# One hybrid decoder layer: where five key tiles, the first gathered rows and the last norm rows stand around the end of the gate table

## The chip, the core and the metric

The kernel runs on one core of one Trainium2 chip. The metric is the device time in microseconds (us) of one execution, as a median of several. TensorE does the matrix products, VectorE (DVE in the rows) elementwise work, ScalarE (ACT) activations and casts, GpSimd (POOL) issues the gathers, and SyncE (SP) issues most of the other transfers. Each engine works through its own queue in order; what an instruction needs from another engine it waits for at its place in that queue, and everything behind it waits too.

## The reference

The input is 512 tokens of 1024 features. The layer mixes the tokens in two ways (a gated linear recurrence and trailing means), adds the result to the residual stream and normalises it to `h`. Then comes the part that the change touches, a channel mixer that looks up experts:

```python
q = (x @ w_query)                       # per head two half queries
sc = einsum(q, sub_keys)                # 8 heads x 2 halves x 128 keys
top_v, top_i = top_k(sc, 16)            # per half, then the best 16 of the sums
expert = i1 * 128 + i2                  # 16384 experts, 8 x 16 = 128 of them per token
gate = softmax(best_v)
act = gelu(einsum('td,tkd->tk', x, u_tab[expert])) * gate
y = einsum('tk,tkd->td', act, v_tab[expert])
h = LN2(alpha*h + y + ple)
```

`u_tab` and `v_tab` are 16384 x 1024 in float32. `ple` is a gated projection of a second input.

## The kernel before

All products are done as three matmuls of split operands (a high part `wh` and the rest `wl`, in a float32 form that TensorE takes): ScalarE casts `wh` from the loaded tile `wraw` (L219), VectorE subtracts to get `wl` (L220), and `mm3` issues lines 123, 124 and 125.

The 512 tokens are four blocks. The first block (NG = 1) gathers its experts' rows: GpSimd fetches, for each of its 128 experts per token, one row per token with an indirect transfer (`issue`, L967), and VectorE multiplies it with `hg` and sums (`consume`, L978, for `u_tab`), later scales and adds (L981, for `v_tab`). The list `todo` has 128 + 128 such steps. The other three blocks (ND = 384 tokens) compute densely over all 16384 experts, as NT = 128 tiles of 128 experts: a key tile is 8 x 3 matmuls of a `u_tab` tile against the tokens (names `fp`), a gelu, a product with the gates (`weigh`, L1003), and 18 matmuls with the `v_tab` tile into six accumulators (`yacc`).

The gates have to be scattered into a dense table `Gd` (24 groups of 16 tokens). That is the loop `for s in range(nq)`, L925, of 96 steps. A step does one `quad` (12 small matmuls, name `pG`, L890) whose operands `oh` and `A` VectorE builds for two quads at a time (`one_hots`, L870 and L876); ScalarE copies the result to a staging tile `stg` (`evacuate`, L897), and after every fourth quad SyncE writes the group to `Gd` in HBM (L899). Every fourth step also advances `selects()` (the choice of experts of the next block on VectorE, names `eq`, `si`, `eidx`), and eight steps do a `base` (L919). Between the quads the loop spreads the key tiles 15 to 51 (`more_u`): `want = left * (s + 1) // nq`, with `left` = 37 tiles x 8 pieces of three matmuls. Their gelu results are parked in HBM (`Hs`, L643).

Behind the loop come `g_load(order[0])`, which reads one slice of the table back, the gates of eight key tiles (`gt`, L666; it needs every group of `Gd`), and the stage with the value products: `LEAD` = 6 key tiles ahead, then for each tile i the load, the key product of tile i + 6, 18 value matmuls, and a share of gathered rows, `budget += len(todo) * ...`, so that the rows are used up near the end.

What sets the order: in this part of the program the instructions stand on every engine as the Python code emits them. `fetch` (L211) loads weight tiles six ahead of the one in use and splits them three ahead; there are three buffers for `wraw` and four for `wh` and `wl`. The pool `vt` has four large buffers that `stg`, the gathered `rows` (two steps in one buffer), and the gain and bias of the last norm (`gain_bias(2)`, names `gb`, L96, L1010) share. At the start of the last stage the kernel before issues `GL` = 4 gathers (L1052).

Of the kernel before, what the change touches and what calls it, by code (L numbers as in the profile page):

```python
# [15 lines left out]
OP = mybir.AluOpType  # L16
# [5 lines left out]
NCK = 8  # L22
# [8 lines left out]
TG = 16  # L31
VG = 8
NG = 1
ND = S - NG * 128
T0 = NG * 128
NS = 52
PRE = 15
UQ = [0, 0, 0] + [1, 0] * 6 + [1]
UP = [1, 1, 1, 0]
TAIL = 4  # L40
OG = 8
NC2 = 60
CS = 2
EARLY = 4
LEAD = 6
# [6 lines left out]
def hybrid_block(ctx, tc, ins, out, dbg=None):  # L52
    nc = tc.nc
# [29 lines left out]
    hres = persist.tile([128, NB, D], FT, name="hres")  # L83
# [5 lines left out]
    def big(name):  # L89
        return vt.tile([128, 4, S], FT, name=name, tag="vt")  # L90
# [88 lines left out]
    order = list(range(NS, NS + VG))  # L179
# [452 lines left out]
    def flush():  # L632
        while late:
            late.pop(0)()
# [14 lines left out]
    def more_u(n):  # L649
        for _ in range(n):  # L650
            if next(spills, 1) is None:
                done[0] += 1
# [9 lines left out]
    def g_load(e, pool):  # L662
# [4 lines left out]
            gts[j] = gt  # L667
        return gts[j][:, :, (e % VG) * TG:(e % VG + 1) * TG]

    with ExitStack() as pb:  # L670
        rt = pb.enter_context(tc.tile_pool(name="rt", bufs=1))
        eqp = pb.enter_context(tc.tile_pool(name="eqp", bufs=3))
# [252 lines left out]
        for s in range(nq):  # L925
            p = quad(s)
            flush()
            if prev:
                evacuate(s - 1, prev)
            prev = p  # L930
            if s % PACE[0] in PACE[1]:
                next(sels, None)
            elif s % 8 == 7 and s < 64:
                base(s // 8)
            if s % (OG // 4) == 0 and s // (OG // 4) + 1 < ND // OG:
                one_hots(s // (OG // 4) + 1)
            want = left * (s + 1) // nq
            more_u(want - given)
            given = want
        evacuate(nq - 1, prev)  # L940
        for _ in sels:
            pass
        g_load(order[0], g0p)
        more_u(NS * NCK)
        flush()


    with ExitStack() as pc:
# [1 line left out]
        gp = pc.enter_context(tc.tile_pool(name="gp2", bufs=3))  # L950
        yacc = [bank("yacc") for _ in range((NB - NG) * 2)]
        gs, acts, vals = {}, {}, {}

        todo = [(0, b, k) for b in range(NG) for k in range(128)] + [(1, b, k) for b in range(NG) for k in range(128)]
        half_n = len(todo) // 2
        got, cnt, pair = {}, [0, 0], [None]

        def issue():
            n = cnt[0]
            if n >= len(todo):  # L960
                return
            kind, b, k = todo[n]
            if n % 2 == 0:
                pair[0] = big("rows").rearrange("p (a b) c -> p a (b c)", a=2)
            r = pair[0][:, n % 2, :]
            got[n] = r
            nc.gpsimd.indirect_dma_start(out=r, out_offset=None, in_=ins["v_tab" if kind else "u_tab"],  # L967
                                         in_offset=bass.IndirectOffsetOnAxis(ap=eidx[:, b, k:k + 1], axis=0))
            cnt[0] += 1

        def consume():
            n = cnt[1]
            if n >= len(todo) or n not in got:
                return
            kind, b, k = todo[n]
            r = got.pop(n)
            if kind == 0:
                nc.vector.scalar_tensor_tensor(r, r, 1.0, hg[:, b, :], op0=OP.mult, op1=OP.mult,  # L978
                                               accum_out=hdot[:, b, k:k + 1])
            else:  # L980
                nc.vector.scalar_tensor_tensor(hres[:, b, :], r, ggate[:, b, k:k + 1], hres[:, b, :],  # L981
                                               op0=OP.mult, op1=OP.add)
            cnt[1] += 1

        def key_load(i):
            if i < NT:
# [20 lines left out]
                acts[i] = split(vs, gs.pop(i), ND, "a", nc.vector)  # L1007

        lnp = pc.enter_context(tc.tile_pool(name="ln2p", bufs=2))
        g2, b2 = gain_bias(2)  # L1010
        lns = {}

        def finish(blk, half):
# [35 lines left out]
            key_product(i)  # L1049
            weigh(i)  # L1050
        split_act(0)
        GL = 4  # L1052
        for _ in range(GL):
            issue()
        share, tot = 0.0, sum(2 if e >= NS else 1 for e in order[:NT - TAIL - EARLY])
        budget = 0.0
        wait_n = 0
        for i in range(NT):
            key_load(i + LEAD + 1)
            split_act(i + 1)  # L1060
            key_product(i + LEAD)
            vals[i] = take()
            if i < NT - TAIL:
                for b in range(NB - NG):
                    values(i, b)
                acts.pop(i), vals.pop(i)
            budget += len(todo) * (2 if order[i] >= NS else 1) / tot
            while budget >= 1:
                budget -= 1
                if cnt[1] == half_n and wait_n < 2:  # L1070
                    if wait_n == 0:
                        nc.scalar.activation(hdot, hdot, AF.Gelu)
                        nc.vector.tensor_mul(ggate, ggate, hdot)
                    wait_n += 1
                    continue
                consume()
                issue()
            weigh(i + LEAD)
            if i == NT - TAIL - 1:
                while cnt[1] < len(todo):  # L1080
                    consume()
                    issue()
                for blk in range(NG):
                    for half in range(2):
                        finish(blk, half)
                    close(blk)
# [64 lines left out]
```

## Time and profile before

| | us |
|---|---|
| median of 3 runs | 1815.38 (1810.57 to 1819.29) |
| the profiled execution, its own time | 1821.71 |
| span of the profiled execution | 1820.0 |
| TensorE busy | 1759.8 |
| VectorE busy | 1302.0 |
| gate loop, first to last quad | 693.7 to 937.6 |

The views used are the page (busy time of each engine), the table of windows (busy time of the engines, granted TensorE clock and DMA share in a stretch, with the number of instructions behind an x), the groups of instructions by line, the chain of work that ended last, and the timelines of single engines. Times inside the execution are counted from the span's start.

### The profile page before, as it was taken

What the parts mean: (1) busy time and instruction counts of PE and PEld (TensorE: products, weight loads), DVE (VectorE), ACT (ScalarE), POOL (GpSimd) and SP (SyncE); (2) the same over time, 40 slices, a digit from 0 to 9 for tenths busy, and PEclk for the clock granted to TensorE, in tenths of its full rate; (3) what the DMA queues carried; (4) which work ended last, traced back from release to release, by engine and by line L of the source; (5) the groups of instructions that cost most, each with busy time, mean ns of one, the idle gap of its engine ahead of it and who ended that gap; (6) DMA issues with size and microseconds to landing.
All of it is one profiled execution on the core that took longest, in us unless ns stands there. A gap on an engine that the chain in (4) does not pass through costs nothing.

```text
span 1820.0 us, 25277 instructions
## 1 busy us (share of the span) xinstructions
PE 1759.8 (97%) x9677; PEld 1539.9 (85%) x9677; DVE 1302.0 (72%) x2332; ACT 748.4 (41%) x1052; POOL 642.0 (35%) x421
## 2 busy tenths in 40 slices
PE   7999999999999999999999999999999999999997
PEld 5777787888788998888988888888878888888886
DVE  6455444234589869999846887887867887878887
ACT  3567754332332355655653343323333332333332
POOL 3532323344345540000012543453433443444450
PEclk9999999999999999999999999999999999999999
DMA  4322222342233335565688999899998999899983
GB/s 145 117 69 70 60 69 87 104 139 93 77 96 115 106 109 174 197 232 192 239 291 277 367 335 375 320 317 360 315 325 291 339 336 323 312 338 325 328 304 105
DMA packets 159694, 399.10 MB, mean 219 GB/s; under 512 B 12882, under 2 KB 75858, under 8 KB 156372
## 3 DMA queue, kind: packets, MB, share of 16 engines
q1 hardware_dynamic: 115220, 253.02, 41.5%
q0 software_dynamic: 36864, 134.23, 20.5%
q10 hardware_dynamic: 7488, 10.23, 1.5%
q8 instruction: 76, 1.25, 0.3%
q14 instruction: 46, 0.38, 0.1%
HBM read 359.94 MB, written 37.49 MB: 218 GB/s over the span
## 4 chain that ended last, share of the span: by engine, by line
PE 77%; DVE 9%; DMA 5%; issue 2%; ACT 2%; ACTq 0%; DVEq 0%; SPq 0%
PE fp L123 14%; PE fp L124 14%; PE fp L125 14%; PE yacc L124 8%; PE yacc L125 8%; PE yacc L123 8%; DMA wraw<-in_v_tab_dram 4%; PE ple L841 3%; DVE A L876 2%; DVE wl L220 2%; PE pG L890 2%; DVE oh L870 2%; DMA wraw<-in_u_tab_t_dram 1%; PE sc L785 1%; PE acc L125 1%
## 5 line engine op out<-in xcount | busy, mean ns | idle before, releaser
L123 PE MATMUL fp<-othi,wh 128*128 128x384 f32 (+1 forms) x1216 | 429.2, 353 | 0.3 <-ACT othi L136 0.3
L125 PE MATMUL fp<-othi,wl 128*128 128x384 f32 (+1 forms) x1216 | 420.7, 346 | 6.2 <-DVE wl L220 6.2
L219 ACT CAST wh<-wraw 128x1024 fp32r<-128x1024 f32 x280 | 294.3, 1052 | 308.1 <-DMA wraw<-in_v_tab_dram 203.9
L124 PE MATMUL fp<-otlo,wh 128*128 128x384 f32 (+1 forms) x1216 | 419.6, 345 | 0.2 <-DVE otlo L137 0.2
L220 DVE TENSOR_TENSOR wl<-wraw,wh 128x1024 fp32r<-128x1024 f32 x246 | 300.4, 1224 | 156.1 <-ACT wh L219 155.6
L967 POOL DMA_INDIRECT rows<-in_u_tab_dram,eidx x128 | 179.6, 1403 | 494.4 <-DVE oh L870 248.3
L123 PE MATMUL yacc<-wh,ah 128*128 128x512 f32 x768 | 301.0, 392 | 6.6 <-ACT wh L219 6.6
L124 PE MATMUL yacc<-wl,ah 128*128 128x512 f32 x768 | 302.6, 394 | 4.0 <-DVE wl L220 4.0
L125 PE MATMUL yacc<-wh,al 128*128 128x512 f32 x768 | 302.0, 393 | 0.0
L967 POOL DMA_INDIRECT rows<-in_v_tab_dram,eidx x128 | 186.9, 1461 | 231.1 <-DVE hres L981 193.3
L119 POOL TENSOR_TENSOR wl<-wraw,wh 128x1024 fp32r<-128x1024 f32 x68 | 167.8, 2471 | 277.3 <-ACT wh L118 277.3
L125 PEld LDWEIGHTS fp<-othi,wl 128*128 128x128 f32 x1216 | 229.4, 189 | 14.4 <-DVE wl L220 6.9
L124 PEld LDWEIGHTS fp<-otlo,wh 128*128 128x128 f32 x1216 | 229.8, 189 | 10.3 <-DVE otlo L137 0.5
L123 PEld LDWEIGHTS fp<-othi,wh 128*128 128x128 f32 x1216 | 229.6, 189 | 10.3 <-ACT othi L136 0.5
L627 ACT ACTIVATE ge<-fp 128x384 f32<-128x384 f32 x128 | 62.9, 492 | 352.8 <-PE fp L125 352.8
L123 PEld LDWEIGHTS yacc<-wh,ah 128*128 128x128 f32 x768 | 145.2, 189 | 36.8 <-ACT wh L219 8.1
L124 PEld LDWEIGHTS yacc<-wl,ah 128*128 128x128 f32 x768 | 145.2, 189 | 35.2 <-DVE wl L220 6.2
L125 PEld LDWEIGHTS yacc<-wh,al 128*128 128x128 f32 x768 | 145.2, 189 | 30.7 <-DVE al L119 0.3
L981 DVE SCALAR_TENSOR_TENSOR hres<-rows,ggate,hres 128x1024 f32<-128x1024 f32 x128 | 164.1, 1282 | 2.4
L978 DVE SCALAR_TENSOR_TENSOR rows<-rows,hg 128x1024 f32<-128x1024 f32 x128 | 151.1, 1219 | 0.7 <-DMA rows<-in_u_tab_dram,eidx 0.7
L123 PE MATMUL fp<-xthi,wh 128*128 128x512 f32 x352 | 142.4, 405 | 1.5 <-DVE q L426 1.5
L118 ACT CAST wh<-wraw 128x1024 fp32r<-128x1024 f32 x68 | 71.1, 1048 | 163.9 <-issue 100.6
(245 smaller groups left out, 2519.5 us busy)
## 6 DMA issues: line engine op xcount, KB each, us to landing
wraw<-in_u_tab_t_dram SPq DMA_DIRECT2D x128, 512.0 KB, 4.9
wraw<-in_v_tab_dram SPq DMA_DIRECT2D x128, 512.0 KB, 7.0
Gd<-stg SPq DMA_DIRECT2D x24, 1024.0 KB, 6.3
gt<-Gd SPq DMA_DIRECT2D x16, 1536.0 KB, 15.5
wraw<-in_w_in_dram SPq DMA_DIRECT2D x44, 512.0 KB, 3.5
Hs<-ge ACTq DMA_DIRECT2D x52, 192.0 KB, 2.7
ge<-Hs SPq DMA_DIRECT2D x52, 192.0 KB, 7.5
wraw<-in_w_query_dram SPq DMA_DIRECT2D x16, 512.0 KB, 3.4
```

The source lines that it names most:

```text
L118: nc.scalar.copy(hi, src)
L119: lo_eng.tensor_sub(lo, src, hi.bitcast(FT))
L123: nc.tensor.matmul(o, a[0], b[0], start=start, stop=False)
L124: nc.tensor.matmul(o, a[0], b[1], start=False, stop=False)
L125: nc.tensor.matmul(o, a[1], b[0], start=False, stop=stop)
L219: f(hi, raw)
L220: g(lo, raw, hi.bitcast(FT))
L627: nc.scalar.activation(ge, p[:, :ND], AF.Gelu)
L841: nc.tensor.matmul(o, a[x], b[y], start=(cc == 0 and blk % 2 == 0 and n == 0), stop=(cc == NCK - 1 and n == 2), skip_group_check=True)
L967: nc.gpsimd.indirect_dma_start(out=r, out_offset=None, in_=ins["v_tab" if kind else "u_tab"], in_offset=bass.IndirectOffsetOnAxis(ap=eidx[ ...
L978: nc.vector.scalar_tensor_tensor(r, r, 1.0, hg[:, b, :], op0=OP.mult, op1=OP.mult, accum_out=hdot[:, b, k:k + 1])
L981: nc.vector.scalar_tensor_tensor(hres[:, b, :], r, ggate[:, b, k:k + 1], hres[:, b, :], op0=OP.mult, op1=OP.add)
```

## The change

Five of the 37 key tiles (`REST`) leave the gate loop and stand behind it, after the load of the first table slice. Four gathers (`AHEAD`) are issued in the loop's step 80 instead of at the start of the last stage; behind the loop four rows are multiplied, each followed by the issue of one more. `for _ in sels` stands in step 80 too. The gain and bias of the last norm are loaded in iteration 6 of the last stage instead of before it. The definitions of `issue` and `consume` move up unchanged; the budget counts 252 rows instead of 256. No arithmetic changes.

```diff
--- before.py
+++ after.py
@@ -38,6 +38,8 @@
 UQ = [0, 0, 0] + [1, 0] * 6 + [1]
 UP = [1, 1, 1, 0]
 TAIL = 4
+REST = 5
+AHEAD = 4
 OG = 8
 NC2 = 60
 CS = 2
@@ -667,6 +669,37 @@
             gts[j] = gt
         return gts[j][:, :, (e % VG) * TG:(e % VG + 1) * TG]
 
+    todo = [(0, b, k) for b in range(NG) for k in range(128)] + [(1, b, k) for b in range(NG) for k in range(128)]
+    half_n = len(todo) // 2
+    got, cnt, pair = {}, [0, 0], [None]
+
...
     with ExitStack() as pb:
         rt = pb.enter_context(tc.tile_pool(name="rt", bufs=1))
         eqp = pb.enter_context(tc.tile_pool(name="eqp", bufs=3))
@@ -934,15 +967,22 @@
                 base(s // 8)
             if s % (OG // 4) == 0 and s // (OG // 4) + 1 < ND // OG:
                 one_hots(s // (OG // 4) + 1)
-            want = left * (s + 1) // nq
+            want = (left - REST * NCK) * (s + 1) // nq
             more_u(want - given)
             given = want
+            if s == nq - TG:
+                for _ in sels:
+                    pass
+                for _ in range(AHEAD):
+                    issue()
         evacuate(nq - 1, prev)
-        for _ in sels:
-            pass
         g_load(order[0], g0p)
-        more_u(NS * NCK)
-        flush()
+        for _ in range(AHEAD):
+            consume()
+            issue()
+        for _ in range(REST):
+            more_u(NCK)
+            flush()
 
 
     with ExitStack() as pc:
@@ -950,37 +990,6 @@
         gp = pc.enter_context(tc.tile_pool(name="gp2", bufs=3))
         yacc = [bank("yacc") for _ in range((NB - NG) * 2)]
         gs, acts, vals = {}, {}, {}
-
-        todo = [(0, b, k) for b in range(NG) for k in range(128)] + [(1, b, k) for b in range(NG) for k in range(128)]
-        half_n = len(todo) // 2
-        got, cnt, pair = {}, [0, 0], [None]
-
...
         def key_load(i):
             if i < NT:
@@ -1007,7 +1016,6 @@
                 acts[i] = split(vs, gs.pop(i), ND, "a", nc.vector)
 
         lnp = pc.enter_context(tc.tile_pool(name="ln2p", bufs=2))
-        g2, b2 = gain_bias(2)
         lns = {}
 
         def finish(blk, half):
@@ -1049,9 +1057,6 @@
             key_product(i)
             weigh(i)
         split_act(0)
-        GL = 4
-        for _ in range(GL):
-            issue()
         share, tot = 0.0, sum(2 if e >= NS else 1 for e in order[:NT - TAIL - EARLY])
         budget = 0.0
         wait_n = 0
@@ -1064,7 +1069,7 @@
                 for b in range(NB - NG):
                     values(i, b)
                 acts.pop(i), vals.pop(i)
-            budget += len(todo) * (2 if order[i] >= NS else 1) / tot
+            budget += (len(todo) - AHEAD) * (2 if order[i] >= NS else 1) / tot
             while budget >= 1:
                 budget -= 1
                 if cnt[1] == half_n and wait_n < 2:
@@ -1076,6 +1081,8 @@
                 consume()
                 issue()
             weigh(i + LEAD)
+            if i == LEAD:
+                g2, b2 = gain_bias(2)
             if i == NT - TAIL - 1:
                 while cnt[1] < len(todo):
                     consume()
```

SyncE's queue around the loop's end, before: the last groups of the gate table are written (`Gd`), the first slice is read back (`gt`), then come the two norm rows (`gb`), the second slice, and key and value tiles (`wraw`).

```order
L899 DMA Gd<-stg 128x2048
L141 DMA wraw<-in_u_tab_t_dram 128x1024
L899 DMA Gd<-stg 128x2048
L666 DMA gt<-Gd 128x24x128
L96 DMA gb<-in_ln_g_dram 128x1024
L96 DMA gb<-in_ln_b_dram 128x1024
L666 DMA gt<-Gd 128x24x128
L141 DMA wraw<-in_u_tab_t_dram 128x1024 x2
L141 DMA wraw<-in_v_tab_dram 128x1024
L141 DMA wraw<-in_u_tab_t_dram 128x1024
```

The same place now:

```order
L932 DMA Gd<-stg 128x2048
L143 DMA wraw<-in_u_tab_t_dram 128x1024
L932 DMA Gd<-stg 128x2048
L668 DMA gt<-Gd 128x24x128
L143 DMA wraw<-in_u_tab_t_dram 128x1024 x5
L668 DMA gt<-Gd 128x24x128
L143 DMA wraw<-in_u_tab_t_dram 128x1024 x2
L143 DMA wraw<-in_v_tab_dram 128x1024
```

Five loads of key tiles now stand between the two slice reads, where the norm rows stood. The norm rows are twenty rows of the list further on in SyncE's queue, among the loads of the last stage (`Hs` is a parked gelu result):

```order
L143 DMA wraw<-in_u_tab_t_dram 128x1024
L143 DMA wraw<-in_v_tab_dram 128x1024
L98 DMA gb<-in_ln_g_dram 128x1024
L98 DMA gb<-in_ln_b_dram 128x1024
L999 DMA ge<-Hs_3537 128x384
L143 DMA wraw<-in_u_tab_t_dram 128x1024
```

There they stand directly ahead of the load of the parked result 3.

VectorE's queue at the loop's end, before: the last operands of the quads, two splits of key tiles, and then the first product with the gates (`ge<-ge,gt`), which needs the slice of the table.

```order
L870 TENSOR_TENSOR oh<-iota_81,iT 128x2048
L876 TENSOR_TENSOR A_8896<-oh,gT 128x1024
L876 TENSOR_TENSOR A_8898<-oh,gT 128x1024
L876 TENSOR_TENSOR A_8900<-oh,gT 128x1024
L220 TENSOR_TENSOR wl<-wraw,wh 128x1024 x2
L1003 TENSOR_TENSOR ge<-ge,gt 128x384
L220 TENSOR_TENSOR wl<-wraw,wh 128x1024
```

The same place now, from the last quads' operands to the first product with the gates:

```order
L903 TENSOR_TENSOR oh<-iota_81,iT 128x2048
L909 TENSOR_TENSOR A_8738<-oh,gT 128x1024
L909 TENSOR_TENSOR A_8740<-oh,gT 128x1024
L909 TENSOR_TENSOR A_8742<-oh,gT 128x1024
L222 TENSOR_TENSOR wl<-wraw,wh 128x1024
L696 SCALAR_TENSOR_TENSOR rows,hdot<-rows,hg 128x1024 x4
L222 TENSOR_TENSOR wl<-wraw,wh 128x1024 x6
L1012 TENSOR_TENSOR ge<-ge,gt 128x384
```

Between the last operands and the first product with the gates stood two splits; now seven splits and the multiplications of four gathered rows (`rows`) stand there.

## Rows read from the trace of the kernel before

**Rows 1.** The page: engine, busy us, share of the span, instructions.

```profile
PE 1759.8 (97%) x9677; PEld 1539.9 (85%) x9677; DVE 1302.0 (72%) x2332; ACT 748.4 (41%) x1052; POOL 642.0 (35%) x421
```

**Rows 2.** The table of windows: the gate loop's two parts, its end, the gap.

```profile
core 0: us, PE busy (x) PEld busy (x) DVE busy (x) ACT busy (x) POOL busy (x), PEclk, DMA share, GB/s
693.70:872.30 178.60, 167.71 (x1451) 153.44 (x1449) 171.72 (x217) 105.44 (x125) 0.00 (x0) 0.99 0.59 202
872.30:937.60 65.30, 65.12 (x588) 60.60 (x586) 53.08 (x64) 41.97 (x49) 2.58 (x2) 1.00 0.69 242
937.60:952.60 15.00, 15.00 (x90) 14.82 (x86) 1.23 (x1) 5.62 (x8) 3.74 (x4) 1.00 1.00 345
952.60:965.00 12.40, 7.56 (x28) 7.42 (x28) 3.77 (x5) 0.32 (x1) 0.00 (x0) 0.72 1.13 340
```

**Rows 3.** Waits of TensorE, 693 to 938: us in total, times, longest us.

```profile
PE pG L890 <- DVE A L876: 10.7, 21, 1.5
```

**Rows 4.** The chain that ended last, at the loop's end: start, us, what.

```profile
938.88 4.51 DMA Gd<-stg
943.46 12.29 DMA gt<-Gd
956.31 1.23 DVE wl L220
957.58 0.69 PE fp L125
958.27 0.32 PE fp L123
```

**Rows 5.** The timeline of VectorE at the gap; in brackets idle before, releaser.

```profile
955.84 0.56 DVE L1003 TENSOR_TENSOR ge<-ge,gt 128x384 f32<-128x384 f32 x1 [12.63 <-DMA gt<-Gd]
```

**Rows 6.** The timeline of TensorE at the gap; in brackets idle before, releaser.

```profile
957.58 0.69 PE L125 MATMUL fp<-othi,wl 128*128 128x384 f32 x1 [4.84 <-DVE wl L220]
```

**Rows 7.** VectorE's groups by line, 693.7 to 872.3: busy, mean ns, idle before.

```profile
L220 DVE TENSOR_TENSOR wl<-wraw,wh 128x1024 fp32r<-128x1024 f32 x27 | 32.9, 1218 | 2.2 <-ACT wh L219 2.1
...
L760 DVE TENSOR_TENSOR gr<-pt,gT 128x128 f32<-128x128 f32 x2 | 0.6, 291 | 2.6 <-ACT gT L759 2.6
```

**Rows 8.** The timeline of ScalarE behind the loop.

```profile
944.11 0.49 ACT L627 ACTIVATE ge<-fp 128x384 f32<-128x384 f32 x1 [2.16 <-PE fp L125]
...
948.27 0.49 ACT L627 ACTIVATE ge<-fp 128x384 f32<-128x384 f32 x1 [2.73 <-PE fp L125]
...
965.09 1.05 ACT L219 CAST wh<-wraw 128x1024 fp32r<-128x1024 f32 x1 [12.18 <-DMA wraw<-in_u_tab_t_dram]
```

**Rows 9.** The timeline of SyncE behind the loop: start, us of issuing.

```profile
943.46 0.38 SPq L666 DMA_DIRECT2D gt<-Gd  x1
943.94 7.47 SPq L96 DMA_DIRECT2D gb<-in_ln_g_dram  x1
...
952.84 7.48 SPq L141 DMA_DIRECT2D wraw<-in_u_tab_t_dram  x2
```

**Rows 10.** The page's DMA issues: median us from issue to landing at the end.

```profile
wraw<-in_u_tab_t_dram SPq DMA_DIRECT2D x128, 512.0 KB, 4.9
```

**Rows 11.** The timeline of GpSimd: the first gathers.

```profile
924.89 1.64 POOL L967 DMA_INDIRECT rows<-in_u_tab_dram,eidx  x1 [248.27 <-DVE oh L870]
926.84 0.94 POOL L967 DMA_INDIRECT rows<-in_u_tab_dram,eidx  x1 [0.30 <-issue]
```

**Rows 12.** The timeline of VectorE beside the first gather.

```profile
923.58 1.23 DVE L870 TENSOR_TENSOR oh<-iota,iT 128x2048 bf16<-128x2048 bf16 x1 [0.38 <-PE pG L890]
924.84 1.89 DVE L876 TENSOR_TENSOR A<-oh,gT 128x1024 bf16<-128x1024 bf16 x3
```

**Rows 13.** The timeline of VectorE: one gathered row multiplied, in the last stage.

```profile
979.57 1.22 DVE L978 SCALAR_TENSOR_TENSOR rows<-rows,hg 128x1024 f32<-128x1024 f32 x1
```

**Rows 14.** The table of windows: the last stage, and its worst 40 us.

```profile
1340.00:1380.00 40.00, 35.79 (x160) 30.68 (x159) 26.32 (x39) 11.48 (x17) 14.87 (x11) 0.91 0.90 310
...
940.00:1800.00 860.00, 843.17 (x4082) 746.82 (x4081) 669.88 (x854) 292.49 (x410) 363.39 (x254) 0.99 0.92 321
```

More of the change, by code (lines that the diff above doesn't have):

```diff
@@ L668, in g_load, with issue, consume @@
         return gts[j][:, :, (e % VG) * TG:(e % VG + 1) * TG]
+    todo = [(0, b, k) for b in range(NG) for k in range(128)] + [(1, b, k) for b in range(NG) for k in range(128)]
+    half_n = len(todo) // 2
+    got, cnt, pair = {}, [0, 0], [None]
+    def issue():
+        n = cnt[0]
+        if n >= len(todo):
+            return
+        kind, b, k = todo[n]
+        if n % 2 == 0:
+            pair[0] = big("rows").rearrange("p (a b) c -> p a (b c)", a=2)
+        r = pair[0][:, n % 2, :]
+        got[n] = r
+        nc.gpsimd.indirect_dma_start(out=r, out_offset=None, in_=ins["v_tab" if kind else "u_tab"],
+                                     in_offset=bass.IndirectOffsetOnAxis(ap=eidx[:, b, k:k + 1], axis=0))
+        cnt[0] += 1
+    def consume():
+        n = cnt[1]
+        if n >= len(todo) or n not in got:
+            return
+        kind, b, k = todo[n]
+        r = got.pop(n)
+        if kind == 0:
+            nc.vector.scalar_tensor_tensor(r, r, 1.0, hg[:, b, :], op0=OP.mult, op1=OP.mult,
+                                           accum_out=hdot[:, b, k:k + 1])
+        else:
+            nc.vector.scalar_tensor_tensor(hres[:, b, :], r, ggate[:, b, k:k + 1], hres[:, b, :],
+                                           op0=OP.mult, op1=OP.add)
+        cnt[1] += 1
     with ExitStack() as pb:
@@ L952, in hybrid_block @@
         gs, acts, vals = {}, {}, {}
-        todo = [(0, b, k) for b in range(NG) for k in range(128)] + [(1, b, k) for b in range(NG) for k in range(128)]
-        half_n = len(todo) // 2
-        got, cnt, pair = {}, [0, 0], [None]
[L958 to L983, printed above, removed]
         def key_load(i):
```

## The prediction

> **What bounds the kernel now.** The page first: TensorE is busy for 97% of the span, VectorE for 72% [rows 1]. Such a share is a mean over stages, so the stages that the change touches come next, in the table of windows [rows 2]. In the first row, quads 0 to 67 of the gate loop, look at VectorE: 171.7 of 178.6 us busy. It builds the operands of the quads, chooses the next blocks' experts and splits the key tiles, and it is all that TensorE's quads wait for [rows 3]: 1451 matmul records in 178.6 us are 8.1 per us, against 588 in 65.3, which is 9.0, in the second row (quads 68 to 95, the same mix of work). There VectorE has 53.1 of 65.3 us, and TensorE is the bound. The third row is key tiles alone at full rate, 90 in 15 us. The fourth is the hole: 28 matmuls in 12.4 us, granted clock 0.72.
>
> The chain of waits says where the hole is from [rows 4]: the last group's write takes 4.51 us, the slice read behind it 12.29, then a split on VectorE, then TensorE. VectorE had idled 12.63 us ahead of the first product with the gates [rows 5], with the split for the fourth early key tile queued behind that product; TensorE stood 4.84 us [rows 6] and came back at 0.32 us a matmul [rows 4], the lower of its two clock levels for about 7 us. So before, three key tiles of cover stand against a wait of 18 us.
>
> **The hole closes: -7.7 us.** The third row's rate is 6 matmuls per us, so 12.4 us hold 74; 28 were done, 46 are missing, 46 / 6 = 7.7 us. One key tile takes 4.16 us, the distance between two gelus [rows 8], so the five moved tiles put 20.8 us of TensorE work between the last quad and the first tile that needs the slice. VectorE's new order has seven splits ahead of the product with the gates where it had two, so the wait for the slice no longer holds a split back: eight tiles, 33 us, stand against 18 us.
>
> **The loop pays: +6.9 us.** Removing 20.8 us from the loop gives 20.8 us back only where TensorE is the bound. The tiles are spread evenly, so 68/96 of it, 14.7 us, leaves quads 0 to 67, and 6.1 us leaves quads 68 to 95. The latter come back in full: 65.3 - 6.1 = 59.2 us is still above VectorE's 53.1. In quads 0 to 67 VectorE sets the pace. Its 27 splits of 1.218 us [rows 7] shrink in the ratio 32 to 37, by 3.6, which is 4.4 us. It also idles for 178.6 - 171.7 = 6.9 us, and 4.7 of these (2.6 and 2.1 us [rows 7]) are waits for ScalarE copies that stand in TensorE's pace and shrink when TensorE comes along faster; the rest are hand-overs that stay. I take half, 3.4 us. So that stretch gets 4.4 + 3.4 = 7.8 us shorter for 14.7 us of work, and 14.7 - 7.8 = 6.9 us are paid again behind the loop. Bounds: all idle time recovered, 14.7 - 4.4 - 6.9 = 3.4; none, 10.3.
>
> **The new place of the load that comes next: +0.5 us.** What is late once the slice is not? The load of the first tile behind the moved five: it now stands in SyncE's queue directly behind the slice read. Count from the last quad's end, T = 937.6. The slice read can't be issued before T + 5.8, as now. The issue after it was held 7.47 us [rows 9]; if that happens again, this load goes out at T + 13.8. It lands 4.9 us later (the median [rows 10]) to 12.2 us later (the ScalarE wait of the load at 952.84, which stood behind two slices and both norm rows [rows 8, 9]). Cast 1.05 and split 1.22 make T + 21 to T + 28. TensorE wants it at the loop's remainder of 2.1 us plus 20.8, T + 22.9. So 0 to 5.4 us; I take 0.5, near the low end, because only one slice stands ahead of it now. The loads behind it have 4.16 us more each.
>
> **The gathers: 0.** Four multiplications of 1.22 us [rows 13] come ahead of the splits behind the loop. They hold those back by 4.9 us, but tiles are split three ahead (12.5 us) and VectorE idles there; nothing is paid. As to the requests, the label promises more than happens: GpSimd runs ahead, and the first pair went out at 924.89 and 926.84 already [rows 11], inside the loop. Issuing four in step 80 moves them by some 30 us against a transfer that nobody waits for. They hold two of the four large buffers from there; the staging tiles lived on two while the gated projection held the others (quads 0 to 63) and the quads waited for nothing but VectorE there [rows 3].
>
> **The last stage: -1.0 us.** It now has 252 rows to fetch instead of 256, 2 MB less, and takes over 1 MB of norm rows: 1 MB at 321 GB/s [rows 14] is 3.3 us of transfer in a stage where TensorE lacks 860.0 - 843.2 = 16.8 us, part of that to transfers. I take 1 us of gain. Bounds: -3.3, and +4.2, if the norm rows, which held SyncE 7.47 us in their old place, open a hole there like the one in the worst 40 us (40.0 - 35.8 [rows 14]).
>
> **The sum.** -7.7 + 6.9 + 0.5 - 1.0 = -1.3 us. The profiled execution took 1821.7 (span 1820.0 and 1.7 around it), 6.3 above the median, so 1820.4 against it and 1814.1 as a median: no change that can be told. The low ends give -7.7 + 3.4 + 0 - 3.3 = -7.6, median 1807.8; the high ends, with 2 us for the load, -7.7 + 10.3 + 2 + 4.2 = +8.8, median 1824.2.
>
> **Rivals.**
> *The loop doesn't pay.* TensorE's gaps there may be a matter of when VectorE's bursts fall, not of its sum, and shorter quads may then let the loop shrink by nearly all 20.8 us. Then -7.7 + 0 + 0 - 1.0 = -8.7, median 1806.7, and 1804.4 with the best last stage. Against it: 172 of 179 us busy leave no room for 14.7 us less. For it: the hand-overs between VectorE's instructions are counted as idle, and records overlap a little. Chance 0.2.
> *The hole comes back one step later* (the slower one). If the load behind the slice lands later than T + 20.6 by 5 us, TensorE stands as long as before and comes back at the lower clock: the 7.7 us are lost again, and -7.7 + 6.9 + 7.7 - 1.0 = +5.9, median 1821.3, slower than before; with the loop's high end 1824.7. It decides at a landing 12 us after issue. For it: TensorE's need at T + 22.9 against T + 21 at best is a margin of 2 us. Chance 0.13.
> *The gathers hold VectorE.* If a gather's issue on GpSimd kept VectorE from starting, four in the loop would cost at most 4 x 1.64 = 6.6 us [rows 11], in quads where VectorE has 59.2 - 51.6 = 7.6 us to spare (its 53.1 less 1.5 for splits), or less in the denser part: up to +6.6 - 1.3 = +5.3, median 1820.7. The row speaks against it: at 924.89 a gather ran 1.64 us beside operand builds of 1.23 and 1.89 us [rows 12], their usual lengths; the gather was the longer one (0.94 alone). By the Trainium skill, SBUF — State Buffer, section "SBUF: two separate sides", VectorE (in some of its modes or with two inputs) and GpSimd take a shared port pair as an exclusive lock, and whichever starts second blocks fully; by that rule a gather that starts first would hold VectorE for its whole length. The trace shows GpSimd stretched by 0.7 us and VectorE not, so half of the rule. Chance 0.07.
>
> **How the numbers follow.** The forecast, no change within its bounds, has 0.6. About 0.5% of the time, 9 us, is what a measurement of this kernel can tell from no change. Faster by more needs the first rival with a good last stage, or all low ends: 0.12. Slower by more needs the second with the loop's high end, or all high ends: 0.08. The rest is 0.80. The range, 8 in 10, reaches from the first rival's time to just short of the high ends: 1806 to 1823.
>
> **What would show it.** In the changed profile the gate loop, first to last quad, should last 243.9 - 13.9 = 230 us; 224 or less speaks for the first rival, 235 or more against the idle time recovered. VectorE should be busy 97% or more in quads 0 to 67, with TensorE at fewer than 8 matmuls per us. Behind the loop TensorE should run from the last quad through eleven key tiles without a wait above 1 us, at full granted clock, and VectorE's wait for the slice should be gone; a wait of TensorE for the split of the sixth tile, with ScalarE waiting for its load, is the second rival. Operand builds longer than 1.23 us in step 80 and behind are the third. I am wrong altogether if the last stage changes by more than 4 us: it is the largest part, and I moved almost nothing in it.

## The result, and the profile after

The changed kernel takes 1829.68 us (median of 4 runs, 1828.0 to 1832.41) against 1816.44 for the kernel before on the same chip: ratio 1.0071, 95% interval 1.0042 to 1.0101. That is slower by 13 us (0.7%), outside the predicted range. The profiled execution has a span of 1826.3 us, 6.3 above that of before.

The page of the changed kernel, the line of [rows 1]: TensorE has five more busy microseconds in a span six longer.

```profile
PE 1764.7 (97%) x9677; PEld 1543.6 (85%) x9677; DVE 1300.9 (71%) x2332; ACT 747.3 (41%) x1052; POOL 636.7 (35%) x421
```

The table of windows of the changed kernel, columns as in [rows 2]: quads 0 to 67, quads 68 to 95, the tiles behind the loop, the new hole, the time at the lower clock.

```profile
692.50:866.60 174.10, 159.75 (x1368) 144.06 (x1366) 168.37 (x214) 99.59 (x118) 0.00 (x0) 0.95 0.55 193
866.60:928.70 62.10, 60.36 (x554) 55.12 (x553) 51.13 (x63) 39.39 (x46) 5.05 (x4) 1.00 0.75 258
928.70:951.10 22.40, 22.40 (x132) 22.26 (x129) 7.57 (x11) 5.96 (x9) 9.67 (x8) 1.00 0.99 341
951.10:957.40 6.30, 0.18 (x2) 0.00 (x0) 0.39 (x1) 1.44 (x2) 0.00 (x0) 0.68 0.98 330
957.40:963.50 6.10, 6.07 (x18) 5.71 (x19) 3.29 (x3) 2.48 (x3) 0.00 (x0) 0.50 0.73 211
```

With 20.8 us of key tiles gone, quads 0 to 67 are only 4.5 us shorter than in [rows 2] and quads 68 to 95 only 3.2. Behind the loop TensorE runs 22.4 us without a gap, then stops again.

**Where the 6.3 us of the profile lie.** For each quad of the loop, the lost time is the distance to the next quad's first matmul, less 0.70 us for its own twelve and 0.1735 for each key matmul between (their spacings where nothing waits). Behind the loop it is what the distance between two matmuls has over the usual one of their kind, up to 985 us (the hole) and from there on (the last stage). Span = first quad's time + three losses + a rest, and the rest is 1069.3 to 1069.5 us in all 14 kernels of this study, so these four numbers hold every difference. (The expectations below use a coarser count that differs by up to 0.5 us.) Beside them, the median of each kernel's runs:

```
kernel                   first  loop  hole  last   span    median  (runs)
before                   693.7  24.7   8.0  24.1  1820.0   1816.4   4
after                    692.5  37.3   9.5  17.6  1826.3   1829.7   4
e1_tiles_only            694.3  37.2   4.9  18.2  1824.0   1821.9  12
e2_no_tiles              693.9  27.0  13.5  21.1  1824.9   1825.3  10
e3_load_first            691.9  37.3   4.2  18.9  1821.8   1825.7   6
e5_shift                 694.1  29.4   7.4  21.3  1821.7   1816.9  12
e6_gathers_late          692.0  37.2   2.4  17.7  1818.8   1824.7  12
e8_weigh_gb_later        693.8  27.1   5.8  19.0  1815.2   1816.0  12
e9_before_shift          691.8  23.8  13.2  21.5  1819.8   1823.7  12
e10_shift_gathers_late   691.9  29.4   1.7  20.1  1812.6   1817.5  12
e11_cast_first           692.2  32.3   7.0  12.2  1813.1   1821.6  12
e12_before_cast_first    693.5  22.5  10.5  17.2  1813.1   1819.7  12
e13_all                  692.0  29.3   3.8  15.1  1809.6   1817.1  12
e14_three_tiles          691.8  26.6   6.7  20.1  1814.7   1816.2  12
```

So in the profiles the loop lost 12.6 us more, the hole 1.5 more, the last stage 6.5 less, the start 1.2 less. Loop and hole together, 14.1, are about the 13.2 us of the medians. Median less loop and hole is between 1779.8 and 1786.7 for all kernels, 1783.7 before and 1782.9 after: the last stage's share in one profile (12 to 24 us) follows no edit that these runs resolve.

**The loop, in the rows.** The table of waits of the changed kernel, TensorE, 693 to 928 (us in total, times, longest); [rows 3] has 10.7, 21 and 1.5:

```profile
PE pG L923 <- DVE A L909: 15.8, 30, 2.3
```

The quads that lost over 0.75 us stand apart in a pattern:

```
before   0, 3, 4, 8, 27, 28, 31, 32, 51, 52, 56, 60
after    0, 3, 4, 12, 16, 24, 27, 28, 29, 36, 40, 48, 51, 52, 60, 64, 72, 78, 84, 90
```

Those at 3, 27 and 51 and just behind are the bursts in which VectorE chooses experts; both kernels have them. New are, but for 29, multiples of 6 (12, 24, 36, 48, 72, 78, 84, 90) and of 8 (16, 40, 64). With 32 tiles over 96 quads a tile now ends exactly ahead of every third quad, and operands are built for every second, so both meet at every sixth. Of the 12.6 us, by the same count, 7.5 lie at the multiples of 6 (60 with them), 1.2 at 16, 40 and 64, and 3.7 at the bursts (quads 3 to 9, 27 to 34, 51 to 59). Why the quads 6, 18, 30, 42, 54 and 66 lose next to nothing, and 16, 40 and 64 something, these rows don't show. The timelines of ScalarE (first two lines), VectorE (next three) and TensorE (last two) at quad 72 of the changed kernel; in brackets idle before, releaser:

```profile
870.01 1.05 ACT L930 COPY stg<-pG 128x512 f32<-128x512 f32 x1 [0.40 <-ACT ge L629]
870.85 1.06 ACT L221 CAST wh<-wraw 128x1024 fp32r<-128x1024 f32 x1
...
871.95 1.23 DVE L222 TENSOR_TENSOR wl<-wraw,wh 128x1024 fp32r<-128x1024 f32 x1 [1.82 <-ACT wh L221]
873.09 1.22 DVE L903 TENSOR_TENSOR oh<-iota,iT 128x2048 bf16<-128x2048 bf16 x1
874.34 1.90 DVE L909 TENSOR_TENSOR A<-oh,gT 128x1024 bf16<-128x1024 bf16 x3
...
875.40 0.50 PE L923 MATMUL pG<-A,oh 128*128 128x128 bf16 x2
876.29 0.73 PE L923 MATMUL pG<-A,oh 128*128 128x128 bf16 x10 [0.38 <-DVE A L909]
```

Read it from the left: a tile has just ended, ScalarE's gelu is over, and the copy of a quad stands in its queue ahead of the cast for the next tile. VectorE, in order, has the split of that cast ahead of the next operands, and idles 1.82 us. The operands come late, and quad 72 waits between its second and third matmul.

At a burst more is lost than before. VectorE's timeline, then TensorE's, at quads 3 and 4 of the changed kernel:

```profile
700.14 2.29 DVE L771 TENSOR_TENSOR eq<-eq,topf 128x2048 bf16<-128x2048 bf16 x1
702.35 1.22 DVE L903 TENSOR_TENSOR oh<-iota,iT 128x2048 bf16<-128x2048 bf16 x1
703.60 1.90 DVE L909 TENSOR_TENSOR A<-oh,gT 128x1024 bf16<-128x1024 bf16 x3
...
704.35 0.29 PE L923 MATMUL pG<-A,oh 128*128 128x128 bf16 x1 [2.27 <-DVE A L909]
...
707.32 0.52 PE L127 MATMUL fp<-othi,wl 128*128 128x384 f32 x1
707.64 0.52 PE L125 MATMUL fp<-othi,wh 128*128 128x384 f32 x1
```

TensorE stood 2.27 us and came back with 0.32 us from matmul to matmul, the lower clock level. The granted clock over such a burst, from the table of windows of the changed kernel:

```profile
700.00:714.00 14.00, 11.08 (x78) 9.87 (x77) 13.86 (x14) 5.25 (x7) 0.00 (x0) 0.76 0.48 162
...
764.00:774.00 10.00, 8.05 (x47) 7.31 (x48) 9.90 (x12) 2.57 (x4) 0.00 (x0) 0.66 0.48 159
...
825.00:834.00 9.00, 7.11 (x55) 6.55 (x55) 8.90 (x11) 2.86 (x4) 0.00 (x0) 0.81 0.46 162
```

In the kernel before, only the first of the three bursts shows a granted clock under 1.00, with 0.87. That TensorE stands longer here because fewer key matmuls lie between the quads would be one reading, but the runs don't bear it out. e2 and e8 below have all 37 tiles in the loop and no wait of TensorE for the operands over 1.5 us, and lose 18.5 and 18.6 us at the bursts, against 15.5 before and 19.2 in the changed kernel. In both the clock falls behind all three bursts. Two of them in the table of windows of e8:

```profile
716.00:724.00 8.00, 5.98 (x40) 5.33 (x39) 7.93 (x11) 4.07 (x5) 0.00 (x0) 0.79 0.60 221
780.00:788.00 8.00, 5.95 (x40) 5.35 (x40) 7.90 (x12) 2.04 (x2) 0.00 (x0) 0.79 0.36 116
```

So the bursts' part of the loss isn't shown to come from the tiles; its cause is open.

**The hole, in the rows.** The chain that ended last in the changed kernel (start, us, what), against [rows 4]:

```profile
935.95 19.91 DMA wraw<-in_u_tab_t_dram
956.01 0.88 issue
956.89 0.49 ACT ge L629
957.43 0.69 PE fp L125
958.12 0.32 PE fp L126
```

It is no longer the slice but the load behind it. The timelines of SyncE (three lines), ScalarE (two), TensorE (one) and GpSimd (first and last of eight gathers) there:

```profile
930.01 0.33 SPq L932 DMA_DIRECT2D Gd<-stg  x1
935.46 0.38 SPq L668 DMA_DIRECT2D gt<-Gd  x1
935.95 24.54 SPq L143 DMA_DIRECT2D wraw<-in_u_tab_t_dram  x5
...
955.94 1.04 ACT L221 CAST wh<-wraw 128x1024 fp32r<-128x1024 f32 x1 [12.45 <-DMA wraw<-in_u_tab_t_dram]
956.89 0.48 ACT L629 ACTIVATE ge<-fp 128x384 f32<-128x384 f32 x1
...
957.43 0.69 PE L125 MATMUL fp<-othi,wh 128*128 128x384 f32 x1 [6.14 <-ACT ge L629]
...
929.43 1.77 POOL L685 DMA_INDIRECT rows<-in_u_tab_dram,eidx  x1 [41.74 <-DMA Hs<-ge]
...
940.30 0.94 POOL L685 DMA_INDIRECT rows<-in_u_tab_dram,eidx  x1 [0.30 <-issue]
```

SyncE stands at the slice until the last group is written, so the first early key tile's load goes out right behind it and lands 19.91 us later. ScalarE waits 12.45 us for it, with the gelus of two finished tiles behind that cast in its queue; with both accumulators (PSUM banks) of the key tiles held, TensorE stops for 6.14 us ([rows 6]: 4.84) and returns at the lower clock. Between 929.43 and 941.24 GpSimd asks for eight gathered blocks. They are not the four of step 80, which had gone out at 874.74 to 886.73, but the next eight. The kernel before and e1 had asked for six in all by then; that fits the norm rows, which held one of the four large buffers there.

### The profile page after: what moved, and what is told of

It is laid out like the page before. It is cut to its first block, busy times and chain, and to the rows that moved or that the text cites. A ratio compares the mean times of both kernels' runs of the same rounds, so it can differ in the third digit from the quotient of the medians.

```text
span 1826.3 us, 25283 instructions
## 1 busy us (share of the span) xinstructions
PE 1764.7 (97%) x9677; PEld 1543.6 (85%) x9677; DVE 1300.9 (71%) x2332; ACT 747.3 (41%) x1052; POOL 636.7 (35%) x421
## 4 chain that ended last, share of the span: by engine, by line
PE 76%; DVE 10%; DMA 5%; ACT 2%; issue 2%; SPq 0%; ACTq 0%; DVEq 0%
PE fp L125 14%; PE fp L126 14%; PE fp L127 13%; PE yacc L126 8%; PE yacc L127 8%; PE yacc L125 8%; DMA wraw<-in_v_tab_dram 3%; DVE A L909 3%; PE ple L874 3%; DVE wl L222 2%; DVE oh L903 2%; DMA wraw<-in_u_tab_t_dram 2%; PE pG L923 1%; PE sc L818 1%; DVE eq L771 1%
## 5 line engine op out<-in xcount | busy, mean ns | idle before, releaser
L685 POOL DMA_INDIRECT rows<-in_u_tab_dram,eidx x128 | 175.7, 1373 | 505.9 <-DVE rows L696 234.1
L126 PEld LDWEIGHTS fp<-otlo,wh 128*128 128x128 f32 x1216 | 230.9, 190 | 10.3 <-DVE otlo L139 0.5
```

The costliest lines, as they stand in the source:

```text
L126: nc.tensor.matmul(o, a[0], b[1], start=False, stop=False)
```

## The experiments

Theory A: the loop pays because of where tiles end (A1), and the hole returns because the load stands behind the slice read. Rival B: the gathers hold that load. Rivals A2 to A4: the sum of VectorE's work, or the order in any such loop.

**The parts alone.** e1 is the kernel before with only the tiles moved, e2 the changed kernel without:

```diff
# e1, from the kernel before
+REST = 5
...
-            want = left * (s + 1) // nq
+            want = (left - REST * NCK) * (s + 1) // nq
...
-        more_u(NS * NCK)
-        flush()
+        for _ in range(REST):
+            more_u(NCK)
+            flush()
# e2, from the changed kernel
-REST = 5
+REST = 0
...
-        for _ in range(REST):
-            more_u(NCK)
-            flush()
+        more_u(NS * NCK)
+        flush()
```

> One part alone: the kernel before with the five key tiles moved behind the loop; the gathers and the norm rows stay where they were. Theory A (the tiles taken out of the loop leave time behind in it, about 13 us, and the hole behind the loop stays because the first key tile's load stands in SyncE's queue behind the slice read): loop 13 longer than wanted, hole about 9 us of lost TensorE time as in the changed kernel, so 1826 to 1831 us against 1816.4 before. Rival B (the hole stays because eight gathered blocks of rows travel beside that load): without the early gathers the load lands 5 to 12 us after its issue, the hole goes (-7.7), and the time is 1819 to 1823 us.

> The other parts alone: the changed kernel with no tile moved; all key tiles stay spread over the loop's 96 quads, the first four gathers are requested in the loop's last quads and multiplied behind the slice read, and the norm rows are loaded later. Theory A (the loss is the loop's): 1814 to 1819 us, about the kernel before, with the loop at 243 us from first to last quad. Rival C (the early gathers or the late norm rows cost the time, in the hole or in the last stage): 1825 to 1830 us. If the gathered rows slow the slice read, the hole is longer than the 15 us between loop end and landing that it had, by up to 8 us.

e1: 1821.91 us, ratio to before 1.003 (1.0009 to 1.0051). e2: 1825.31 us, 1.0042 (1.0028 to 1.0057). Each half alone costs, and both times are those of the rivals, not of theory A. e1's loop loses 37.2 us, as after, so that loss needs neither the early gathers nor the late norm rows; its load lands 14.6 us after its issue instead of 19.9 and the hole falls to 4.9: the rival's time, but not its closed hole. The slice in e1 lands 13.9 us after its issue at 938.84, so the load comes in 1.2 us behind it. e2's loop loses 2.3 us more than before, all of it at the bursts, and its hole grows to 13.5, as the expectation's last sentence said. The chains of e1 (first line) and e2 (second), then VectorE's timeline of e2, the wait that [rows 5] shows with 12.63:

```profile
939.33 14.62 DMA wraw<-in_u_tab_t_dram
...
946.32 17.49 DMA gt<-Gd
...
963.89 0.56 DVE L1011 TENSOR_TENSOR ge<-ge,gt 128x384 f32<-128x384 f32 x1 [18.16 <-DMA gt<-Gd]
```

The slice took 17.5 us with eight gathers beside it, and 12.3 before with four [rows 4].

**Queue or gathers.** e3 asks for the slice two tiles later; e6 puts the gathers back:

```diff
# e3, from the changed kernel
-        g_load(order[0], g0p)
         for _ in range(AHEAD):
             consume()
             issue()
-        for _ in range(REST):
+        for r in range(REST):
             more_u(NCK)
             flush()
+            if r == 1:
+                g_load(order[0], g0p)
# e6, from the changed kernel
-AHEAD = 4
+AHEAD = 0
...
         split_act(0)
+        for _ in range(4):
+            issue()
```

> The changed kernel with the read of the slice asked for two key tiles later, so that two key tile loads stand ahead of it in SyncE's queue; the gathers are multiplied and asked for at the same place, ahead of it. Theory A (the first load waits behind the slice read): the load now lands ahead of the need, TensorE goes through the eleven key tiles with no wait over 1 us, and the hole's 9.3 us of lost time become 0 to 2: 1820 to 1824 us against 1829.7. Rival B (the gathers' traffic holds the load): the load still lands 15 us or more after its issue, and the time stays at 1826 to 1830. Rival D: the slice itself, or the load behind it, now comes late: a wait of VectorE for the slice beyond the eleven tiles, 1826 or more as well, but at another place in the trace.

> The changed kernel with the first gathers requested and multiplied where the kernel before has them; the five moved tiles and the later norm rows stay. Theory B (eight gathered blocks in the air beside the slice read lengthen it and the load behind it, 14 us without them and 20 with them): the first key tile's load lands within 15 us, the lost TensorE time behind the loop is 4 to 5 us instead of 9.4, the loop loses 37 us as before this edit, and the time is 1819 to 1824 us against 1829.7. Theory A (the order in SyncE's queue alone): the load still lands 18 us or more after its issue, 1826 to 1831.

e3: 1825.66 us, 1.0056 (1.0038 to 1.0074), 4 us off the changed kernel; e6: 1824.66 us, 1.0039 (1.0022 to 1.0055), 5 us off. Neither theory alone: in e3 two loads go ahead of the slice, and the hole shrinks to 4.2, not to 0 to 2, because the third load, again behind the slice, lands 17.6 us after issue (rival D's place). The DMA issues of e3 at 933 to 934 (us to landing at the end), and its chain:

```profile
wraw<-in_u_tab_t_dram SPq DMA_DIRECT2D x1, 512.0 KB, 9.1
...
941.59 17.62 DMA wraw<-in_u_tab_t_dram
```

The first load, among the same eight gathers but ahead of the slice, lands after 9.1 us. The slice itself takes 20.0 us there, and the third load lands 1.3 us behind it. In e6 the load stands where the change has it. The timelines of SyncE and ScalarE in e6:

```profile
937.42 0.38 SPq L668 DMA_DIRECT2D gt<-Gd  x1
937.91 17.34 SPq L143 DMA_DIRECT2D wraw<-in_u_tab_t_dram  x5
...
950.70 1.04 ACT L221 CAST wh<-wraw 128x1024 fp32r<-128x1024 f32 x1 [7.77 <-DMA wraw<-in_u_tab_t_dram]
```

It lands 12.7 us after issue, 7 us sooner than with the early gathers, and the hole is 2.4, smaller than B's 4 to 5; the time is just above B's range. Not all of the 7 us is a gain: the last group's write took 8.0 us here (929.41 to the slice's issue) and 5.5 in the changed kernel, so counted from the last quad's end the load lands 4.7 us sooner. So the queue makes the load late and the gathers make it later; together they are the 19.9.

**Where tiles end.** e5 gives the pieces out two earlier in the changed kernel, e9 in the kernel before:

```diff
# e5, from the changed kernel
-            want = (left - REST * NCK) * (s + 1) // nq
+            want = min(left - REST * NCK, (left - REST * NCK) * (s + 1) // nq + 2)
# e9, from the kernel before
-            want = left * (s + 1) // nq
+            want = min(left, left * (s + 1) // nq + 2)
```

> The changed kernel with the key pieces in the loop given out two pieces earlier: the same pieces, the same operations, only a tile's last piece no longer stands right ahead of a quad but two pieces (about 1 us) before it. Theory A1 (of what the loop did not give back, the 0.83 us lost at the quads 72, 78, 84 and 90 is the chain tile end, gelu, copy, cast, split, operand build, because tiles end exactly at every third quad): these four losses go or shrink to under 0.3, the last 28 quads take 58.5 to 60 us instead of 62.1, and the time is 1826 to 1828 us. Rival A2 (VectorE's or ScalarE's work as a sum sets that pace, wherever the boundaries fall): the last 28 quads still take 61.5 to 62.5 us, and the time is 1829 to 1831.

> The kernel before with only the loop's key pieces given out two pieces earlier. Theory A1 (a tile that ends right ahead of a quad costs, and with five tiles fewer that happens at every third quad, in the kernel before only now and then): the loop loses 20 to 25 us, 24.4 in the kernel before, and the time is 1813 to 1818 us. Rival A3 (pieces given out earlier help any such loop, whatever the tiles' phase): the loop gains 6 us or more, as it did in the changed kernel, and the time is 1806 to 1811.

e5: 1816.89 us, 1.0005 (0.9989 to 1.0022): the whole loss is gone, more than expected. Its profile accounts for 10.0 of the 12.8 us (loop 7.9, hole 2.1). The loop's gain lies at the multiples of 6, which lose 2.2 us instead of 9.0; the bursts still lose 19.4 (19.2 without the edit). The table of windows of e5, the same two stretches as above:

```profile
694.10:864.10 170.00, 157.57 (x1374) 142.93 (x1373) 167.88 (x214) 102.61 (x119) 0.00 (x0) 0.97 0.58 199
864.10:923.50 59.40, 59.17 (x554) 54.79 (x553) 55.29 (x69) 39.49 (x45) 7.67 (x6) 1.00 0.76 274
```

The same work takes 170.0 and 59.4 us instead of 174.1 and 62.1, and VectorE's wait for the cast in quads 68 to 95 all but goes. That wait in the changed kernel, then in e5, from the tables of waits (us, times, longest):

```profile
DVE wl L222 <- ACT wh L221: 10.5, 5, 2.2
```

```profile
DVE wl L222 <- ACT wh L221: 1.9, 3, 0.6
```

The sum of work (A2) is therefore not what set that pace. In the kernel before, where tiles end anywhere, the same edit changes the loop from 24.7 to 23.8, as A1 said, so A3 falls. e9 is slower all the same, 1823.74 us, 1.0036 (1.002 to 1.0052), above both its ranges: its hole is 13.2. The chain of e9 against [rows 4]:

```profile
937.13 9.51 DMA Gd<-stg
946.71 11.66 DMA gt<-Gd
```

The last group's write took 9.51 us instead of 4.51. Two gathers were asked for at 935.11 and 936.35, just ahead of that write, and none in the kernel before between 926.84 and 939.43. That fits the gathers' traffic as the cause; no run takes it apart.

**The chain itself.** e11 (changed kernel) and e12 (kernel before) leave the tiles where they are and turn round ScalarE's order:

```diff
             flush()
-            if prev:
-                evacuate(s - 1, prev)
-            prev = p
...
             given = want
+            if prev:
+                evacuate(s - 1, prev)
+            prev = p
```

> The changed kernel with one order turned round in the loop: a quad's copy out of PSUM is given to ScalarE after the quad's key pieces and not ahead of them, so that the cast of the next key tile stands ahead of that copy on ScalarE; pieces, tiles and gathers are where the change has them. Theory A1 in its strict form (the loss at a tile's end is the chain gelu, copy, cast, split, operand build, and the 1.05 us copy in it is what makes it too long): the 0.83 us at the quads 72, 78, 84 and 90 shrink to under 0.2, the loop loses 29 to 33 us instead of 37, and the time is 1822 to 1826 us. Rival A4 (the chain is long enough without the copy, only the tile's place against the quad matters): the loop still loses 35 to 38 us and the time is 1828 to 1831.

> The kernel before with that same order turned round, as a control: if the copy ahead of the cast costs only where tiles end at every third quad, the loop loses 23 to 27 us as it does in the kernel before (24.4), and the time is 1814 to 1818 us. If it costs everywhere, the loop loses under 21 us and the time is 1808 to 1813.

The same quad 72 in e11, ScalarE and VectorE:

```profile
867.83 1.05 ACT L221 CAST wh<-wraw 128x1024 fp32r<-128x1024 f32 x1 [0.40 <-ACT ge L629]
...
868.90 1.23 DVE L222 TENSOR_TENSOR wl<-wraw,wh 128x1024 fp32r<-128x1024 f32 x1 [0.97 <-ACT wh L221]
```

e11: 1821.6 us, 1.002 (1.0001 to 1.0039). The cast now stands right behind the gelu, and VectorE idles 0.97 us instead of 1.82. The losses at 72, 78, 84 and 90 are gone (quads 68 to 95 lose 1.9 us instead of 5.0), so the copy in the chain is the cause there. In quads 0 to 67, 30.4 of 32.2 us stay, where the shift left 27.1: there an earlier cast helps less than a tile that ends elsewhere, perhaps because VectorE is full. e12: 1819.72 us, 1.0007 (0.999 to 1.0025), loop 22.5, both a little outside their ranges: little to gain where tiles don't end in step.

**Both out, and two tries at better.** e10 is e5 with the gathers of e6; e13 adds the order of e11. e8 covers the slice in the kernel before without moving a tile; e14 is e13 with `REST = 3` and e8's later products:

```diff
# e8, from the kernel before (norm rows loaded as in the change)
             key_product(i)
-            weigh(i)
+            if i >= 3:
+                weigh(i - 3)
+        for i in range(LEAD - 3, LEAD):
+            weigh(i)
```

> The changed kernel with both causes taken out: the key pieces given out two earlier and the gathers where they were. If the two add up (loop 7.8 of lost time, hole 4 to 5), the time is 1809 to 1814 us, under the kernel before; if the gathers' place changes nothing once the loop ends earlier, it stays at 1816 to 1819.

> The changed kernel with the pieces two earlier, the gathers where they were, and the cast ahead of the copy. If shift and order cure the same loss, the loop loses 28 to 30 us as with the shift alone and the time is 1815 to 1819 us; if they add up, it loses 24 to 27 us and the time is 1810 to 1814.

> Another way to cover the slice read, with no tile taken from the loop and the gathers where they were: the kernel before with the first six key tiles weighed three tiles later, so that VectorE splits the fourth and fifth ahead of its wait for the slice, and with the norm rows loaded later. If the hole was VectorE's in-order wait and the norm rows' place in SyncE's queue (7.5 us held), TensorE loses under 2 us behind the loop instead of 8.5, the loop takes the 243 us of the kernel before, and the time is 1807 to 1811 us. If the loads behind the slice land late all the same, the hole moves one or two tiles later and the time is 1814 to 1819.

> A version meant to beat both: three tiles moved instead of five, the first six key tiles weighed three tiles later, the gathers where they were, the norm rows later, pieces two earlier, the cast ahead of the copy. By the lost TensorE time: loop 24 to 27 us, hole 1 to 4, so 1809 to 1814 us; if the load behind the slice lands late again, the hole is 5 to 8 and the time 1814 to 1819.

e10: 1817.46 us, 1.0004 (0.9985 to 1.0022); e13: 1817.13 us, 1.0012 (0.9992 to 1.0031); e8: 1816.04 us, 0.999 (0.9973 to 1.0006); e14: 1816.23 us, 0.9997 (0.9977 to 1.0017). None beats the kernel before. Shift and order cure the same loss (29.3 in e13, 29.4 with the shift alone). e14's loop came as expected (26.6), but its hole is 6.7, and the time is that of the late load. e8's hole moved one load on, as its second expectation has it; its chain:

```profile
952.85 12.06 DMA wraw<-in_u_tab_t_dram
964.99 1.05 ACT wh L219
```

Open: e10's hole is 5.7 us smaller than e5's, and the time is the same (1817.46 against 1816.89). Either the last stage takes it back or one profile each misleads; these runs can't tell.

## Why the prediction was wrong, step by step

**The hole closes, -7.7: wrong, +1.5.** The mechanism named went away: VectorE's wait for the slice [rows 5] is gone, and five tiles do cover the slice read. TensorE ran out 22.4 us after the last quad's end, as the step's own count had it (22.9). What failed is the next term, the **load behind the slice, +0.5**: it was issued at T + 7.3 (935.95 less 928.7), earlier than the 13.8 I put, but took 19.91 us to land where I allowed 4.9 to 12.2. The upper bound came from a load behind two slices and the norm rows [rows 8, 9], but with fewer gathers in the air. This is the second rival, with its condition met (a landing over 12 us after issue) and its price about right (the 7.7 lost again; 9.5 measured). I gave it 0.13. The slice ahead of it was mis-sized with it: 12.3 us before, 17.5 to 20.0 with eight gathers beside it (e2, e3), and the load lands right behind the slice.

**The gathers, 0: wrong.** Their multiplication cost nothing and VectorE's builds kept their lengths beside gathers (three in 1.90 us at 874.34, and 1.22 us at 876.16), so the third rival falls. GpSimd's timeline of the changed kernel there:

```profile
874.74 1.31 POOL L685 DMA_INDIRECT rows<-in_u_tab_dram,eidx  x1 [199.31 <-DVE oh L903]
876.35 1.84 POOL L685 DMA_INDIRECT rows<-in_u_tab_dram,eidx  x1 [0.30 <-issue]
```

But "a transfer that nobody waits for" shares the way with one that somebody does: the load lands 12.7 us after issue without the early gathers and 19.9 with them (e6, after), the slice 12.3 and 17.5 (before, e2). In the hole that is 5.5 to 7.1 us (before to e2, after to e6). The step counted the four requests of step 80; the eight beside the slice are those that follow them. By the Trainium skill, DMA: Bandwidth & Descriptors, section "Issuing engines are not separate DMA queues", transfers begun by SyncE, ScalarE and GpSimd run on the same 16 DMA engines and interleave; the trace agrees, with its DMA share at 0.98 to 1.00 from 928.7 to 957.4 us. The prediction did not weigh that rule.

**The loop pays, +6.9: mis-sized, 12.6.** The bounds ended at 10.3. The step argued from sums: 7.8 us come back in quads 0 to 67, 6.1 in quads 68 to 95. Measured were 4.5 and 3.2 (the loop lasts 235.4 us from first to last quad, which the prediction had as the mark against its idle time); with the tiles' ends moved by two pieces (e5), 8.6 and 5.9. In the step's own terms for quads 0 to 67, VectorE's work shrank by 3.4 us (4.4 put) and its idle time by 1.2 (3.4 put); in e5 by 3.8 and 4.8. So the sums were about right for a loop without the new lock-step, with some luck, as half of the idle time was a guess, and the step that failed is the one not made: that 37 tiles over 96 quads fall anywhere and 32 fall on every third. "The latter come back in full", since VectorE has 53.1 of 59.2 us, overlooked that an engine with time to spare can still be late when it takes its work in order. The bursts with their lower clock, 3.7 of the 12.6, were in no term; as e2 and e8 lose 3.0 more there than before with no tile moved, that part isn't shown to be a price of the tiles.

**The last stage, -1.0: not told apart.** The profiles say -6.5, which by my own bound of 4 us would be wrong altogether; the medians leave -0.8 once loop and hole are taken off, a difference that itself spreads by 7 us over the kernels, and single profiles spread by 12 us whatever the edit. The later norm rows show no stall of their own.

**The sum.** -7.7 + 6.9 + 0.5 + 0 - 1.0 = -1.3 became, by the profiles, +1.5 + 12.6 - 0.8 (what the medians leave, not measured by itself) = 13.3. The rival that came true would have given +5.9; the loop's 5.7 above its term are most of the rest.

## What to carry to other kernels

When work is taken out of a loop in which two streams are interleaved by a ratio, work out the new ratio: if the pieces now end in step with the loop, each hand-over between in-order engines falls on the same spot every time, and a shift of a piece or two can be worth as much as taking the work out gave back (here 7.9 us against 7.7). A load placed behind a large read in the same queue is late by that read, and transfers "that nobody waits for" requested in the same microseconds add to it; count the bytes in the air, not only the queue. A cover moved ahead of one wait has to be checked against the load that comes next behind it.

## What was not expected of the hardware

A 512 KB load that lands 4.9 us after its issue as a median [rows 10] took 9.1 us among eight gathers but ahead of the slice read (e3), 12.7 behind the slice read with four gathers around it (e6), and 19.9 with both. A wait of TensorE of 2.27 us inside the busy loop was followed by the lower clock level, 0.32 us a matmul instead of 0.17; in the kernel before, where no such wait is over 1.5 us [rows 3], the clock fell at the first burst alone, and in e2 and e8, with the same longest wait, behind all three. By the Trainium skill, SBUF — State Buffer, section "SBUF: two separate sides", VectorE and GpSimd lock a shared port pair against each other; here again only GpSimd's gather was the longer (1.31 us at 874.74 and 1.84 at 876.35 against 0.94), and VectorE's operand builds were not, although the second and third of the three from 874.34 on began while the first gather ran; there the measurement differs from the rule.
